# Projecting unnormalised columns that the host laid out, and testing for overfull experts between the last w1 and w3

## The chip, the cores and the metric

The kernel runs on one core of one Trainium2 chip. A core has a matrix engine (PE; its weight loads are listed apart as PEld), a vector engine (DVE), a scalar engine (ACT), a general engine (POOL) and a queue engine (SP) that issues most transfers (DMA). Each engine runs its own list of instructions in order, and semaphores let them wait for each other. The metric is the device time of one execution in microseconds (us); lower is better.

## The reference

One decoder block on 512 tokens of width 1024, in float32, followed by a final norm:

```python
h = rmsnorm(x, attn_norm_w[l])
z = h @ w_in[l]
hq, hf, hi, hg, cq, ckv, kr, gate_a, gate_b = jnp.split(z, split_idx, axis=-1)
...
q = (rmsnorm(c_q, q_norm_w) @ w_uq).reshape(B, S, MLA_HEADS, MLA_QK_DIM)
kv = (rmsnorm(c_kv, kv_norm_w) @ w_ukv).reshape(B, S, MLA_HEADS, MLA_NOPE + MLA_VDIM)
k_pe = apply_rope(k_rope_raw, cos, sin)
...
x = x + y @ w_out[l]
h = rmsnorm(x, ffn_norm_w[l])
x = x + hierarchical_moe(h, ...)
...
y = x * lax.rsqrt(jnp.mean(x * x, axis=-1, keepdims=True) + EPS) * w      # rmsnorm
hid = jax.nn.silu(xb @ w1[e]) * (xb @ w3[e])                              # each expert
return (hid @ w2[e]) * wts[:, None]
```

`cq` has 384 columns and `ckv` with `kr` 320. The mixture of experts has 64 experts of width 512, and each token goes to two. An expert may draw more tokens than one slot list of the kernel holds; it is then called overfull, and a further round has to work off the rest.

## The kernel before

**Order of the work.** The kernel goes through three stages. The *head* (`latent`, L284 to L488) computes the norm, the 384 query columns `cq` and the 320 key and value columns `ckv`/`kr`, and from them the compressed queries (`cqT`), keys (`ckT`) and the values. The *mixers* project and run the latent attention and the recurrent mixer head by head, then the router chooses experts. The *experts* run in 16 blocks of 4 experts each; their weights, 24 MB a block, come through a ring of 22 slots (`RING`) that SP fills as slots come free.

**Products.** A float32 product is made of three reduced-precision ones (`mm3`): each operand is split into a high part (a cast on ACT) and a low part (a subtraction on DVE or POOL), and high by high, high by low and low by high are summed. A tile whose name ends in h or l (`hTh`, `hTl`, `cqwh`, `cqwl`) is such a part.

**The head.** Four tiles of 128 tokens of x are loaded (`xt`). For each one ACT squares it, DVE makes the reciprocal root (`rms_scale`), the tile is scaled, PE transposes it in blocks of 128 (`tr<-dg,xt`, `tr<-cst,xt`), DVE multiplies by the norm's gains (`hf`, L385), ACT casts the high part (`hTh`) and DVE makes the low part (`hTl`, L387). Then PE makes 24 matmuls of 128x384 for this token tile (`c<-cqwh,hTh` and its like: the *query projection*), and after the four tiles 24 of 128x320 a tile (the *key projection*, into `z` and `c`). POOL makes the low parts of the key weights (`ckwl`). The four results are normalised (`xt<-c`), transposed and split into `cqh`/`cql` (`columns`, L429 to L435), and 36 matmuls of 128x512 make the rotary queries (`rotary_queries`, `c<-cqwh,cqh`). After these come the transposes for `ckT`, and then the values (L654, `z<-whi,hTh`).

**The last block of experts.** `block(..., last=True)` makes the 64 matmuls of w1 into `h1`, the 64 of w3 into `h3`, then `spread` (the weights that bring rows back to tokens) and `finish_open`, then the product of both (`t`, DVE L1165), its transposes (`ga<-cst,t`, L1168) and `hid` (ACT L1170). Then `more_rounds` (L1081 to L1085) tests whether an expert is overfull. With these inputs the test is false. On each engine it is a load of the number `ri` into a register (`TENSOR_LOAD`, L1083) and a jump over the body of the overflow rounds (`COMPARE_BRANCH`, L1084), which on PE holds some 230 matmuls:

```python
        nr = nc.values_load(ri[0:1, 0:1], min_val=0, max_val=S // CAP)
        with tc.If(nr > 1):
            self.overflow(Slots(self.pair(len(self.order) + 6)), mps, mp, nr, self.pos, self.e32, self.wts)
```

Then `end` works through w2 in four strips of columns, 512, 256, 128 and 128 wide (`STRIPS`): 16 groups of matmuls into `y`, a copy, four matmuls back to tokens (`cb`, `ga`), additions on DVE, squares on ACT, gains on POOL, and after the last strip the final norm and the stores. SP issues the strips' loads at L887, and passes its own test only after the last of them.

Of the kernel before, what the change touches and what calls it, by code (L numbers as in the profile page):

```python
# [10 lines left out]
F32 = mybir.dt.float32  # L11
# [11 lines left out]
H = 8  # L23
# [53 lines left out]
class Trunk:  # L77
# [48 lines left out]
    def run(self):  # L126
# [3 lines left out]
        nc.scalar.dma_start(out=cst[:, 0:128], in_=a["cf"][:, 0:128])  # L130
# [153 lines left out]
    def latent(self, st, gl, hT, wp):  # L284
# [5 lines left out]
        cqT = [mp.tile([128, 3, S], F32R, name=f"cq{i}") for i in "hl"]  # L290
# [3 lines left out]
        ckT = [mp.tile([128, 2, S], F32R, name=f"ck{i}") for i in "hl"]  # L294
        kpT = [mp.tile([128, S], F32R, name=f"kp{i}") for i in "hl"]
        qpT = mp.tile([128, H, S], F32R, name="qpT")
        scale = float((NOPE + ROPE) ** -0.5)
        with tc.tile_pool(name="c", bufs=1, reuse_waits="tile") as cp, tc.tile_pool(name="cps", bufs=4, space=PSUM, reuse_waits="tile") as cps:
            wk_hl = [cp.tile([128, KT, CW - QR], F32R, name=f"ckw{i}") for i in "hl"]
            gra = cp.tile([8, 128], F32, name="gra")  # L300
            grb = cp.tile([38, 128], F32, name="grb")
            r2 = lambda ap: ap.rearrange("o (k p) -> (o k) p", p=128)
            xt = [cp.tile([128, D], F32, name="xt", bufs=4) for _ in range(T)]

            def load_x(t):
                nc.sync.dma_start(out=xt[t], in_=a["x"][0, t * 128:(t + 1) * 128])

            def weights(c0, w, hl, eng):
                raw = cp.tile([128, KT, w], F32, name="craw")
                hi, lo = hl or [cp.tile([128, KT, w], F32R, name=f"cqw{i}") for i in "hl"]  # L310

                def load(q):
                    nc.sync.dma_start(out=raw[:, 2 * q:2 * q + 2],
                                      in_=w_in[q * 256:(q + 1) * 256, C0 + c0:C0 + c0 + w]
                                      .rearrange("(k p) c -> p k c", p=128))

                def high(kt):
                    nc.scalar.copy(out=hi[:, kt], in_=raw[:, kt])

                def low(kt):  # L320
                    eng.tensor_sub(out=lo[:, kt], in0=raw[:, kt], in1=hi[:, kt])
                return hi, lo, load, high, low

            load_x(0)
            nc.scalar.dma_start(out=gra, in_=r2(a["attn_norm_w"]))
            wq = weights(0, QR, None, nc.vector)
            wq[2](0)
            wq[2](1)
            load_x(1)
            wq[2](2)  # L330
            wq[2](3)
            load_x(2)
            load_x(3)
            wk = weights(QR, CW - QR, wk_hl, nc.gpsimd)
            for q in range(4):
                wk[2](q)
            nc.sync.dma_start(out=self.cst[:, 128:384], in_=a["cf"][:, 128:384])
# [3 lines left out]
            for r0, r1, key in ((0, 16, "hg_lower_bound"), (16, 19, "mla_q_norm_w"), (19, 21, "mla_kv_norm_w"),  # L341
                                (21, 22, "hg_out_norm_w"), (22, 30, "ffn_norm_w")):
                nc.sync.dma_start(out=grb[r0:r1], in_=r2(a[key]))
            nc.sync.dma_start(out=grb[30:38], in_=a["final_norm_w"].rearrange("(k p) -> k p", p=128))
# [4 lines left out]
            ps = cps.tile([128, 8], F32, name="tr", bufs=2)  # L349
            nc.tensor.transpose(ps, gra, ident[0:8, 0:8])  # L350
            nc.vector.tensor_copy(out=gT[:, 0:8], in_=ps)

            def project(ps, w, t):
                ts = slice(t * 128, (t + 1) * 128)
                for kt in range(KT):
                    self.mm3(ps, [hT[0][:, kt, ts], hT[1][:, kt, ts]], [w[0][:, kt], w[1][:, kt]],
                             kt == 0, kt == KT - 1)


            c_sb, cacc = [], []  # L360

            def stats(t):
                return self.rms_scale(sm, xt[t], D, scr)

            def columns_of(t, rs):
                ts = slice(t * 128, (t + 1) * 128)
                if t == 0:
                    dg = cp.tile([128, 128], F32, name="dg")
                    ready = nc.vector.tensor_scalar(out=dg, in0=ident, scalar1=rs, scalar2=None, op0=OP.mult)
                    with tc.issue_after(ready.ins):  # L370
                        for kt in range(4):
                            wq[4](kt)
                else:
                    nc.scalar.activation(xt[t], xt[t], AF.Copy, scale=rs)
                for half in range(2):
                    ps = cps.tile([128, 4, 128], F32, name="tr", bufs=2)
                    for i in range(4):
                        kt = half * 4 + i
                        if t == 0:
                            self.mm(ps[:, i], xt[t][:, kt * 128:(kt + 1) * 128], dg, True, True)  # L380
                        else:
                            nc.tensor.transpose(ps[:, i], xt[t][:, kt * 128:(kt + 1) * 128], ident)
                    ks = slice(half * 4, half * 4 + 4)
# [4 lines left out]
                return cast, low  # L388

            rs = [stats(0)]  # L390
            for kt in range(4):
                wq[3](kt)
            cast, low = columns_of(0, rs[0])
            with tc.issue_after(cast.ins):
                rs.append(stats(1))
                for kt in range(4, KT):
                    wq[3](kt)
            with tc.issue_after(low.ins):
                for kt in range(4, KT):
                    wq[4](kt)  # L400
            for t in range(T):
                if t + 2 < T:
                    rs.append(stats(t + 2))
                if t + 1 < T:
                    cast, low = columns_of(t + 1, rs[t + 1])
                ps = cps.tile([128, QR], F32, name="c")
                project(ps, wq, t)
                cacc.append(ps)
            with tc.issue_after(cast.ins):
                for kt in range(KT):  # L410
                    wk[3](kt)
                    wk[4](kt)
            nc.vector.tensor_copy(out=self.identr, in_=ident)
            for t in range(T):
                rs = self.rms_scale(sm, cacc[t], QR, scr[:, :QR])
                c_sb.append(cp.tile([128, CW - ROPE], F32, name="xt", bufs=4))
                nc.scalar.activation(c_sb[t][:, :QR], cacc[t], AF.Copy, scale=rs)
            kr = cp.tile([128, T, 2, ROPE], F32, name="kr")
            cacc = []
            for t in range(T):  # L420
                ps = zps.tile([128, CW - QR], F32, name="z") if t < 2 else cps.tile([128, CW - QR], F32, name="c")
                project(ps, wk, t)
                cacc.append(ps)
            ps = cps.tile([128, 38], F32, name="tr", bufs=2)
            nc.tensor.transpose(ps, grb, ident[0:38, 0:38])
            nc.vector.tensor_copy(out=gT[:, 8:46], in_=ps)
# [10 lines left out]
            vw = self.value_weights(wp, 0)  # L437
            for r in range(3):
                columns(r, cqT, 0)
            cos, sin = self.angles(cp, pi_)  # L440
            qraw = self.rotary_queries(cp, cps, cqT)
            for t in range(T):
                rs = self.rms_scale(sm, cacc[t][:, :KVR], KVR, scr[:, :KVR])
                nc.scalar.activation(c_sb[t][:, QR:], cacc[t][:, :KVR], AF.Copy, scale=rs)
                nc.scalar.copy(out=kr[:, t, 0], in_=cacc[t][:, KVR:])
# [415 lines left out]
    def prefetch(self, n, eng):  # L861
        goal = min(self.nchunk + n, len(self.order))
        while self.nchunk < goal:
# [12 lines left out]
            elif (i - 16) in self.STRIPS:  # L876
# [3 lines left out]
                n = 512 // w if c0 + w < D else 1  # L880
# [193 lines left out]
    def more_rounds(self, mps):  # L1074
# [9 lines left out]
        with tc.If(nr > 1):  # L1084
            self.overflow(Slots(self.pair(len(self.order) + 6)), mps, mp, nr, self.pos, self.e32, self.wts)  # L1085
# [56 lines left out]
    def block(self, wk, mps, slot, wts, chunk, ready=None, last=False):  # L1142
# [3 lines left out]
        h1 = mps.tile([128, FF], F32, name="h1")  # L1146
        h3 = mps.tile([128, FF], F32, name="h3")
        for i, hp in enumerate((h1, h3)):
            c = chunk(i * 8)
            for kt in range(KT):  # L1150
                for g in range(4):
                    self.mm(hp[32 * g:32 * g + 32], xT[:, kt, 32 * g:32 * g + 32], c(g, kt * 512, 512),
                            kt == 0, kt == KT - 1)
        if ready:
# [161 lines left out]
```

## Time and profile before

| | |
|---|---|
| median of 3 runs | 1607.35 us (1606.48 to 1608.43) |
| the profiled execution | 1605.74 us |
| span of its trace | 1604.0 us (1.74 us lie around it) |
| PE busy, DVE, ACT, POOL | 87%, 37%, 21%, 15% of the span |
| mean transfer rate | 285 GB/s |
| granted PE clock | 0.943 of full speed |

A busy share is a mean over stages with different limits: the head waits for small things, the mixers for PE, most of the expert blocks for transfers. So what an edit is worth is read in its own stage.

### The profile page before, as it was taken

The page shows a single profiled execution, that of the slowest core. Times are in us where ns is not written, and L with a number is a line of the kernel's source. Part 1 is how long each engine was busy: PE and PEld are TensorE (multiplying, and loading weights), DVE is VectorE, ACT ScalarE, POOL GpSimd, SP SyncE. Part 2 cuts the span into 40 slices and gives each one's busy share as a digit, 9 for nine tenths or more (in the row PEclk, how much of TensorE's full clock was granted, in tenths as well). Part 3 has the DMA queues.
Part 4 walks back from the last instruction along what each step waited for, and adds up shares of the span by engine and source line. Part 5 has one row for each costly group of instructions (what it writes and reads, how often), then busy time and mean ns, then how long its engine had stood idle before and what let it go on. Part 6 is the DMA issues. An engine that isn't in the chain of part 4 may idle for free.

```text
span 1604.0 us, 20359 instructions
## 1 busy us (share of the span) xinstructions
PE 1387.9 (87%) x8282; PEld 844.5 (53%) x8282; DVE 592.5 (37%) x1453; ACT 344.6 (21%) x762; POOL 247.8 (15%) x272
## 2 busy tenths in 40 slices
PE   7999999999999999988887788688779779779784
PEld 6878887878788889934243133133223223323322
DVE  7767677686853333621210211111111112012023
ACT  6455523223332223410100000000000000000012
POOL 2021233223000000021111011011012011011012
PEclk9999999999999999998998899898899899889898
DMA  6111222222153338599999999999999999999995
GB/s 219 29 52 51 61 67 66 66 66 66 40 186 104 92 93 328 225 402 430 425 430 429 430 427 428 430 430 427 429 430 429 429 429 429 428 430 428 428 417 175
DMA packets 124766, 456.34 MB, mean 285 GB/s; under 512 B 11854, under 2 KB 93436, under 8 KB 97532
## 3 DMA queue, kind: packets, MB, share of 16 engines
q1 hardware_dynamic: 121852, 454.52, 70.5%
q8 instruction: 67, 1.10, 0.3%
q10 hardware_dynamic: 2816, 0.47, 0.2%
q14 instruction: 31, 0.25, 0.0%
HBM read 452.87 MB, written 2.10 MB: 284 GB/s over the span
## 4 chain that ended last, share of the span: by engine, by line
PE 58%; DMA 26%; DVE 8%; ACT 3%; issue 2%; POOL 1%; SPq 1%; ACTq 0%; POOLq 0%; DVEq 0%
DMA ck<-in_expert_w 24%; PE z L82 13%; PE h L82 10%; PE y L82 10%; PE ga L1111 7%; PE yacc L82 5%; PE wop L82 2%; PE mx L82 2%; PE z L654 1%; PE cb L82 1%; PE sc L82 1%; DVE rs_u L105 1%; PE lv L82 1%; PE o L82 1%; SPq L887 1%
## 5 line engine op out<-in xcount | busy, mean ns | idle before, releaser
L82 PE MATMUL h<-ck,xT 128*32 128x512 f32 x2048 | 311.7, 666 | 123.9 <-DMA ck<-in_expert_w 109.3
L82 PEld LDWEIGHTS h<-ck,xT 128*32 128x32 f32 x2048 | 74.7, 120 | 347.5 <-issue 165.0
L1130 POOL TENSOR_SCALAR t<-cst,slb,wts 128x128 f32<-128x128 f32 x64 | 50.4, 792 | 964.5 <-PE ga L1111 710.0
L1191 DVE TENSOR_TENSOR x<-cb,x 128x512 f32<-128x512 f32 x120 | 83.0, 691 | 290.0 <-PE cb L82 290.0
L82 PE MATMUL y<-ck,hid 128*32 128x512 f32 (+2 forms) x1088 | 171.3, 584 | 16.2 <-ACT hid L1170 9.4
L91 POOL TENSOR_TENSOR wlo<-wraw,whi 128x1024 fp32r<-128x1024 f32 (+3 forms) x52 | 97.6, 1878 | 267.8 <-ACT whi L90 208.2
L82 PE MATMUL z<-hTh,whi 128*128 128x512 f32 x320 | 128.1, 400 | 5.5 <-ACT vh L658 5.4
L1111 PEld LDWEIGHTS ga<-t,wo 128*128 128x128 f32 x1024 | 117.1, 192 | 25.5 <-issue 24.1
L82 PE MATMUL z<-hTh,wlo 128*128 128x512 f32 x320 | 126.9, 397 | 0.0
L82 PE MATMUL z<-hTl,whi 128*128 128x512 f32 x320 | 126.7, 396 | 0.0
L1111 PE MATMUL ga<-t,wo 128*128 128x128 f32 x1024 | 123.2, 278 | 1.2 <-DVE t L1108 1.2
L82 PE MATMUL cb<-xT,owT 128*128 128x512 f32 (+2 forms) x256 | 120.9, 603 | 2.4 <-DVE xT L1207 2.2
L90 ACT CAST whi<-wraw 128x1024 fp32r<-128x1024 f32 (+3 forms) x84 | 77.4, 922 | 173.0 <-PE z L82 93.2
L1165 DVE TENSOR_TENSOR t<-h,t 128x512 f32<-128x512 f32 x16 | 11.1, 692 | 257.9 <-PE h L82 257.9
L82 PEld LDWEIGHTS y<-ck,hid 128*32 128x32 f32 x1088 | 43.7, 111 | 111.2 <-issue 91.6
L82 PEld LDWEIGHTS cb<-xT,owT 128*128 128x128 f32 x256 | 40.3, 188 | 83.5 <-DVE x L1191 46.9
L1187 ACT COPY xT<-y 128x512 f32<-128x512 f32 x30 | 17.6, 585 | 258.5 <-PE y L82 258.5
L1170 ACT COPY hid<-ga 128x512 f32<-128x512 f32 x16 | 9.4, 585 | 293.1 <-PE ga L1168 293.1
L82 PEld LDWEIGHTS z<-hTh,whi 128*128 128x128 f32 x320 | 60.9, 190 | 18.4 <-ACT vh L658 6.0
L1164 DVE TENSOR_TENSOR t<-h,t 128x512 f32<-128x512 f32 x16 | 11.1, 692 | 156.4 <-ACT t L1163 156.4
L82 PEld LDWEIGHTS z<-hTh,wlo 128*128 128x128 f32 x320 | 60.8, 190 | 12.5
L82 PEld LDWEIGHTS z<-hTl,whi 128*128 128x128 f32 x320 | 60.8, 190 | 11.8
(349 smaller groups left out, 2161.2 us busy)
## 6 DMA issues: line engine op xcount, KB each, us to landing
ck<-in_expert_w SPq DMA_DIRECT2D x164, 2048.0 KB, 34.2
ck<-in_expert_w SPq DMA_DIRECT2D x52, 1024.0 KB, 32.4
wraw<-in_w_in SPq DMA_DIRECT2D x48, 512.0 KB, 3.9
wraw<-in_w_branch_mla SPq DMA_DIRECT2D x8, 512.0 KB, 3.7
wraw<-in_w_branch_hgrn SPq DMA_DIRECT2D x8, 512.0 KB, 3.6
wo<-in_w_out SPq DMA_DIRECT2D x8, 512.0 KB, 6.0
xt<-in_x SPq DMA_DIRECT2D x4, 512.0 KB, 6.6
wraw<-in_mla_w_ukv SPq DMA_DIRECT2D x16, 128.0 KB, 2.5
```

Of the source, the lines that this page charges most:

```text
L82: self.nc.tensor.matmul(ps, lhsT=l, rhs=r, start=start, stop=stop)
L90: self.nc.scalar.copy(out=hi, in_=src)
L91: (eng or self.nc.vector).tensor_sub(out=lo, in0=src, in1=hi)
L105: nc.vector.tensor_mul(out=u, in0=u, in1=v)
L654: nc.tensor.matmul(ps[t // 2][:, t % 2], lhsT=L[l], rhs=R[r], start=(kt == 0 and n == 0 and t % 2 == 0), stop=(kt == KT - 1 and n == 2), s ...
L887: eng.dma_start(out=at(ft), in_=w2[ft])
L1111: nc.tensor.matmul(ps[kt // 4][:, kt % 4], lhsT=self.h2[t][:, kt], rhs=oh[:, t], start=(t == 0 and kt % 4 == 0), stop=(t == T - 1), skip_g ...
L1130: nc.gpsimd.tensor_scalar(out=ow[:, t], in0=iota, scalar1=slot(t, 0), scalar2=wts[:, t, 0:1], op0=OP.is_equal, op1=OP.mult)
L1164: nc.vector.tensor_mul(out=sg, in0=rows(h1), in1=sg)
L1165: nc.vector.tensor_mul(out=sg, in0=rows(h3), in1=sg)
L1187: nc.scalar.copy(out=ysb[:, hs], in_=y[half])
L1191: nc.vector.tensor_add(out=self.x2[:, t, hs], in0=ps, in1=self.x2[:, t, hs])
```

## The change

The change has two parts.

**The head.** The host hands in x transposed (`xT`), the two weight slices (`w_cq`, `w_ck`) and all gain vectors (`gains`) in the layout that the chip wants. PE then projects gain times x, without the norm's scale of each token; the scale comes in later, as the scale of the copies that read the results. The loop of the query projection runs over the 8 blocks of 128 features outside and the 4 token tiles inside. x itself is still loaded, for its squares. The normalised `hT`, which the values and later heads need, is made after the key projection from `xT`, gains and the scales spread over all partitions (`rsb`). The low parts of the key weights move from POOL to DVE. The parts of gain times x live in tiles that are free until later (`qpT`, `cqh`, `cql`, `ckh`, and ring slot `ck0` for `xT`).

**The tail.** In the last block `spread`, `finish_open` and `more_rounds` move from behind the matmuls to between those of w1 and those of w3. The overflow body gets other ring slots, since w3 now still stands in the ones that it used, and another PSUM tile for its own `h1`; the last strip packs two pieces into a slot.

```diff
-            def columns_of(t, rs):
...
-                    ps = cps.tile([128, 4, 128], F32, name="tr", bufs=2)
...
-                    hf = cp.tile([128, 4, 128], F32, name="hf", bufs=2)
-                    nc.vector.tensor_mul(out=hf, in0=ps, in1=gT[:, ks, None].to_broadcast([128, 4, 128]))
-                    cast = nc.scalar.copy(out=hT[0][:, ks, ts], in_=hf)
-                    low = nc.vector.tensor_sub(out=hT[1][:, ks, ts], in0=hf, in1=hT[0][:, ks, ts])
...
+            cacc = [cps.tile([128, QR], F32, name="c") for _ in range(T)]
+            for kt in range(KT):
+                g = gT[:, kt:kt + 1]
+                nc.scalar.activation(xgh[:, kt], xT[:, kt], AF.Copy, scale=g)
+                nc.vector.scalar_tensor_tensor(out=low(kt), in0=xT[:, kt], scalar=g, in1=xgh[:, kt],
+                                               op0=OP.mult, op1=OP.subtract)
+                self.split(qraw_[:, kt], wq[0][:, kt], wq[1][:, kt])
+                for t in range(T):
+                    project(cacc[t], wq, t, kt)
...
+            rs = scales([x[:, :] for x in xt], D)
+            for kt in range(KT):
+                self.split(kraw_[:, kt], wk[0][:, kt], wk[1][:, kt])
...
+            sq = scales(cacc, QR, rs)
...
+            for kt in range(KT):
+                hf = cp.tile([128, S], F32, name="hf", bufs=2)
+                nc.vector.scalar_tensor_tensor(out=hf, in0=xT[:, kt], scalar=gT[:, kt:kt + 1], in1=rsb,
+                                               op0=OP.mult, op1=OP.mult)
+                self.split(hf, hT[0][:, kt], hT[1][:, kt])
...
+            sk = scales([c[:, :KVR] for c in cacc], KVR, rs)
...
-                n = 512 // w if c0 + w < D else 1
+                n = 512 // w if c0 + w < D else 2
...
-            self.overflow(Slots(self.pair(len(self.order) + 6)), mps, mp, nr, self.pos, self.e32, self.wts)
+            self.overflow(Slots(self.pair(len(self.order) + 4)), mps, mp, nr, self.pos, self.e32, self.wts)
...
-        for i, hp in enumerate((h1, h3)):
+        hps = []
+        for i in range(2):
+            if i == 1 and last:
+                owT = self.spread(wk, mps, slot, wts)
+                self.finish_open(wk, mps)
+                self.more_rounds(mps)
...
-        owT = self.spread(wk, mps, slot, wts)
-        if last:
-            self.finish_open(wk, mps)
+        if not last:
+            owT = self.spread(wk, mps, slot, wts)
...
-        if last:
-            self.more_rounds(mps)
```

On PE, near the end of the program, the test stood behind the transposes of the product `t`, and the first strip of w2 (`y`) came after the body that it jumps over:

```order
L82 MATMUL h_10108<-ck_9908,xT 32x512 x2
L82 MATMUL h_10108<-ck_9981,xT 32x512 x2
L1168 MATMUL ga<-cst,t_10225 128x128 x4
L1083 TENSOR_LOAD ri
L1084 COMPARE_AND_BRANCH
L1269 COMPARE_AND_BRANCH
```

Now it stands behind the last matmuls of w1 (`h_9998`):

```order
L82 MATMUL h_9998<-ck_9756,xT 32x512
L82 MATMUL h_9998<-ck_9791,xT 32x512
L1041 TENSOR_LOAD ri
L1042 COMPARE_AND_BRANCH
L1232 COMPARE_AND_BRANCH
```

and the rows behind the body begin with those of w3 (`h_10436`), with no jump from there to `y`:

```order
L1042 UNCONDITIONAL_BRANCH
L82 MATMUL h_10436<-ck_9793,xT 32x512 x2
L82 MATMUL h_10436<-ck_9796,xT 32x512 x2
```

So whatever the jump costs PE now lies ahead of w3 and not ahead of w2. On DVE, in the head, the work that makes `hT` stood inside the query projection, tile by tile:

```order
L385 TENSOR_TENSOR hf<-tr,gT 128x512 x2
L102 SCALAR_TENSOR_TENSOR rs_u<-rs_y,rms_v 128x1
L108 TENSOR_SCALAR rs_y<-rms_v 128x1
L387 TENSOR_TENSOR hTl<-hf,hTh 128x4x128
L114 SCALAR_TENSOR_TENSOR rs_y<-rs_u,rs_y 128x1
```

It now stands in one piece between the scales and the splits `cql` that the rotary queries wait for (`ck` is the tile of `xT`):

```order
L91 TENSOR_TENSOR hTl<-hf,hTh 128x512 x2
L377 SCALAR_TENSOR_TENSOR hf<-ck_101,gT,rsb 128x512 x2
L471 TENSOR_SCALAR ang<-ang 128x128
L91 TENSOR_TENSOR cqwl<-craw,cqwh 128x1536
L91 TENSOR_TENSOR hTl<-hf,hTh 128x512 x2
L377 SCALAR_TENSOR_TENSOR hf<-ck_101,gT,rsb 128x512 x2
L388 SCALAR_TENSOR_TENSOR cql<-tr,gT,cqh 128x512
L91 TENSOR_TENSOR hTl<-hf,hTh 128x512 x2
L388 SCALAR_TENSOR_TENSOR cql<-tr,gT,cqh 128x512 x2
```

So the first `cql` is now queued behind six of the eight `hTl` and all eight `hf`.

## Rows read from the trace of the kernel before

**Rows 1.** The page's chain that ended last, by engine and line.

```profile
DMA ck<-in_expert_w 24%; PE z L82 13%; PE h L82 10%; PE y L82 10%; PE ga L1111 7%; PE yacc L82 5%; PE wop L82 2%; PE mx L82 2%; PE z L654 1%; PE cb L82 1%; PE sc L82 1%; DVE rs_u L105 1%; PE lv L82 1%; PE o L82 1%; SPq L887 1%
```

**Rows 2.** Windows: length, busy by engine, then PE clock, transfer share, GB/s.

```profile
400.00:600.00 200.00, 198.42 (x954) 163.15 (x953) 102.94 (x207) 63.98 (x134) 3.56 (x3) 1.00 0.35 103
640.00:660.00 20.00, 19.52 (x167) 19.31 (x166) 9.88 (x49) 8.95 (x18) 0.00 (x0) 1.00 0.50 197
```

**Rows 3.** PE's timeline in the head: start, length, line, operation, idle before.

```profile
5.50 0.24 PE L350 MATMUL tr<-cst,gra 8*128 8x8 f32 x1 [5.50 <-DMA gra<-in_attn_norm_w]
7.98 3.78 PE L82 MATMUL tr<-dg,xt 128*128 128x128 f32 x16 [2.24 <-DVE dg L369]
13.15 0.44 PE L82 MATMUL c<-cqwh,hTl 128*128 128x384 f32 x1 [0.65 <-DVE hTl L387]
...
22.06 0.34 PE L82 MATMUL c<-cqwh,hTh 128*128 128x384 f32 x1
...
25.70 0.34 PE L82 MATMUL c<-cqwh,hTh 128*128 128x384 f32 x1
...
36.21 0.31 PE L82 MATMUL z<-ckwh,hTh 128*128 128x320 f32 x1
...
50.14 0.30 PE L82 MATMUL c<-ckwh,hTl 128*128 128x320 f32 x1
...
54.48 0.79 PE L82 MATMUL c<-cqwh,cqh 128*128 128x512 f32 x1 [0.38 <-ACT cqh L433]
...
64.66 1.03 PE L431 MATMUL tr<-cst,xt 128*128 128x128 f32 x8
65.45 0.36 PE L654 MATMUL z<-whi,hTh 128*128 128x256 f32 x1
```

**Rows 4.** DVE's groups by shape, 0 to 85 us: busy, mean ns, idle before.

```profile
L387 DVE TENSOR_TENSOR hTl<-hf,hTh 128x512 fp32r<-128x512 f32 x8 | 7.2, 906 | 1.5 <-ACT hTh L386 1.4
L385 DVE TENSOR_TENSOR hf<-tr,gT 128x512 f32<-128x512 f32 x8 | 5.3, 684 | 1.2 <-PE tr L82 1.2
```

**Rows 5.** ACT's groups by shape, 0 to 85 us: the load of the exponential's table.

```profile
L483 ACT ACT_TABLE_LOAD x1 | 1.3, 1283 | 0.0
```

**Rows 6.** PE's timeline in the last block.

```profile
1544.29 10.76 PE L82 MATMUL h<-ck,xT 128*32 128x512 f32 x94
...
1559.04 5.32 PE L82 MATMUL h<-ck,xT 128*32 128x512 f32 x26 [1.43 <-DMA ck<-in_expert_w]
1565.23 0.63 PE L1168 MATMUL ga<-cst,t 128*128 128x128 f32 x4 [0.88 <-DVE t L1165]
1572.58 5.39 PE L82 MATMUL y<-ck,hid 128*32 128x512 f32 x32 [6.73 <-DMA ck<-in_expert_w]
```

**Rows 7.** The test's source lines, by engine (q: its sequencer): ns, starts in us.

```profile
L1083 PEldq TENSOR_LOAD <-ri x1: 490/490/490, 1565.2 to 1565.2; - x1
```

```profile
L1084 PEldq COMPARE_BRANCH  x1: 6426/6426/6426, 1565.8 to 1565.8; - x1
...
L1084 ACTq EVENT_SEMAPHORE  x1: 17/17/17, 1570.5 to 1570.5; - x1
```

**Rows 8.** Source line L425 in the head: PE's sequencer and its matmul.

```profile
L425 PEldq EVENT_SEMAPHORE  x2: 51/51/51, 47.7 to 47.8; - x2
...
L425 PE MATMUL tr<-cst,grb x1: 250/250/250, 50.4 to 50.4; 38*128 38x38 f32 x1
```

**Rows 9.** Windows in the last block, columns as in the second group.

```profile
1560.00:1562.00 2.00, 2.00 (x16) 0.50 (x12) 0.00 (x0) 0.00 (x0) 0.00 (x0) 0.50 1.01 387
1568.00:1570.00 2.00, 0.00 (x0) 0.00 (x0) 0.00 (x0) 0.00 (x0) 0.00 (x0) 0.84 1.04 332
...
1581.00:1582.00 1.00, 1.00 (x4) 0.38 (x2) 0.83 (x2) 0.80 (x3) 0.37 (x1) 1.00 0.19 58
```

**Rows 10.** The first strip's last load: its issue (chain), its landing (DMA issues).

```profile
1554.48 2.24 SPq L887
```

```profile
ck<-in_expert_w SPq DMA_DIRECT2D x1, 1024.0 KB, 15.0
```

More of the change, by code (lines that the diff above doesn't have):

```diff
@@ new lines, in latent @@
+            ident, rings = self.ident, self.rings
+            nc.scalar.dma_start(out=gT, in_=a["gains"])
+            nc.scalar.dma_start(out=self.cst, in_=a["cf"][:, 0:384])
+            xT = rings["n"].tile([128, KT, S], F32, name="ck0")
+            xgh = mp.tile([128, H, S], F32R, name="qpT")
+            xgl = [mp.tile([128, n, S], F32R, name=name) for n, name in ((3, "cqh"), (3, "cql"), (2, "ckh"))]
+            low = lambda kt: xgl[kt // 3][:, kt % 3]
+            xt = [cp.tile([128, D], F32, name="xt", bufs=4) for _ in range(T)]
@@ L338, in latent @@
+            wk = [cp.tile([128, KT, CW - QR], F32R, name=f"ckw{i}") for i in "hl"]
+            for k0 in range(0, KT, 4):
+                nc.sync.dma_start(out=kraw_[:, k0:k0 + 4], in_=a["w_ck"][:, k0:k0 + 4])
             nc.sync.dma_start(out=cst2, in_=a["cf"][:, 384:544])
@@ L390, in latent @@
[L390 to L400, printed above, removed]
-            for t in range(T):
[L402 to L413, printed above, removed]
+                self.mm3(ps, [xgh[:, kt, ts], low(kt)[:, ts]], [w[0][:, kt], w[1][:, kt]], kt == 0, kt == KT - 1)
+            cacc = [cps.tile([128, QR], F32, name="c") for _ in range(T)]
[5 more added lines that the diff above has]
+                self.split(qraw_[:, kt], wq[0][:, kt], wq[1][:, kt])
+                for t in range(T):
+                    project(cacc[t], wq, t, kt)
@@ new lines, in scales @@
+            def scales(src, width, rs=None):
+                ss, v = [cp.tile([128, T], F32, name=f"{i}{width}") for i in ("ss", "sv")]
+                for t in range(T):
+                    nc.scalar.activation(scr[:, 0:width], src[t], AF.Square, accum_out=ss[:, t:t + 1])
+                for _ in range(2 if rs is not None else 0):
+                    nc.vector.tensor_mul(out=ss, in0=ss, in1=rs)
+                nc.vector.tensor_scalar(out=v, in0=ss, scalar1=RS / width, scalar2=RS * EPS, op0=OP.mult, op1=OP.add)
+                y = self.rsqrt(sm, v, T)
+                nc.vector.tensor_mul(out=ss, in0=y, in1=rs) if rs is not None else nc.vector.tensor_copy(out=ss, in_=y)
+                return ss
@@ L414, in latent @@
+            rsb = cp.tile([128, S], F32, name="rsb")
+            nc.scalar.copy(out=rsb, in_=ps.rearrange("p t j -> p (t j)"))
+            c_sb = []
+            sq = scales(cacc, QR, rs)
             for t in range(T):
-                rs = self.rms_scale(sm, cacc[t], QR, scr[:, :QR])
                 c_sb.append(cp.tile([128, CW - ROPE], F32, name="xt", bufs=4))
-                nc.scalar.activation(c_sb[t][:, :QR], cacc[t], AF.Copy, scale=rs)
+                nc.scalar.activation(c_sb[t][:, :QR], cacc[t], AF.Copy, scale=sq[:, t:t + 1])
@@ L1140, in spread, with block @@
         return owT
[L1142 removed]
+    def block(self, wk, mps, slot, wts, chunk, ready=None, last=False, other=False):
         nc, ident, iota = self.nc, self.ident, self.iota
         xT = ready or self.gather(wk, mps, slot)
[L1146 to L1148 removed]
+        hps = []
[4 more added lines that the diff above has]
+                self.more_rounds(mps)
+            hp = mps.tile([128, FF], F32, name="cb", bufs=2) if other and i == 0 else \
+                mps.tile([128, FF], F32, name=("h1", "h3")[i])
+            hps.append(hp)
             c = chunk(i * 8)
@@ L1296, with laid_out @@
         "final_norm_w"]
+def laid_out(inputs):
+    rows = lambda m: np.asarray(m).reshape(KT, 128, -1).transpose(1, 0, 2)
+    w = np.asarray(inputs["w_in"])[0]
+    vectors = [np.asarray(inputs[n]).reshape(-1, 128) for n in
+               ("attn_norm_w", "hg_lower_bound", "mla_q_norm_w", "mla_kv_norm_w", "hg_out_norm_w", "ffn_norm_w",
+                "final_norm_w")]
+    return [("xT", rows(np.asarray(inputs["x"])[0].T)), ("w_cq", rows(w[:, C0:C0 + QR])),
+            ("w_ck", rows(w[:, C0 + QR:C0 + CW])), ("gains", np.concatenate(vectors).T)]
 def kernel(**inputs):
```

100 lines of the change are left out of this document (23 added, 77 removed).

## The prediction

> **What bounds the kernel now.** I read the page's chain first. A quarter of the span waits for expert weights, and most of the rest is PE [rows 1]. Then I cut the span into windows. Between 400 and 600 us PE is busy for 198.4 of 200 us, so the mixers run at PE's pace. From 640 to 660 us, in the router, transfers use only half of their time: the ring is full and waits for PE to begin on the experts [rows 2]. So if the head ends earlier, the mixers, the router and the stream of weights all move earlier by the same amount. I read the head from PE's timeline [rows 3] and the costs from the groups of DVE and ACT [rows 4, 5]. I read the tail from PE's timeline in the last block, and from the test's own lines [rows 6, 7].
>
> In the tail the reader should see one thing. The transposes of `t` end at 1565.9, and `hid` follows within 0.6 us, but `y` starts only at 1572.58. The row names a DMA as the releaser. The test's line shows another cause: PE's jump over the overflow body begins at 1565.84 and takes 6.43 us, to 1572.27 [rows 6, 7]. ACT pays too: it is done with `hid` at about 1566.5, and its next instruction, the one behind its jump, is at 1570.5, 4 us later. So the jump stalls its engine.
>
> **The head, step by step.** Before, PE first waits for a small load (5.5 us), then for the norm of the first tile (7.98 to 11.8 are transposes), runs at its full pitch from 13.15 and ends the query projection at 36.2 [rows 3]. The 96 matmuls of 128x384 have a pitch of 0.173 us (21 steps from 22.06 to 25.70), so 16.6 us of that is work; transposes and waits are the rest. The key projection has a pitch of 0.147 (95 steps from 36.21 to 50.14).
>
> After, nothing stands ahead of the first matmul but one block of `xT` and `w_cq`, the gains, and a copy and a cast of 1.1 us on ACT. The gains are a small load like the one that landed at 5.5, so PE starts between 4.5 and 6.6; I take 5.6. Before, 5.2 us went by from PE's first real work to its full pitch. If this holds, PE runs at half rate until 10.8: 15 matmuls of 0.346. The other 81 take 14.0, to 24.8. DVE needs some 1.2 us per block for the two low parts (one 512 wide, at `hf`'s 0.68, and one 384 wide, by its width), less than PE's 2.1, so it is in time. With 0.6 us of friction the query projection ends at 25.4. The key projection takes 14.1, and 0.8 us more because the splits of its weights queue on ACT behind the squares of the results. It ends at 40.3, against 50.3: 10 us earlier.
>
> DVE doesn't keep that. Eight `hf` at 0.68, eight `hTl` at 0.68 to 0.91, one wide split (1.8 by its width), three `cql` (2.2 by the same width and one operand more) and some 25 small operations of 0.2 stand in its list from the scales to the last `cql` [rows 4]: 5.5 + 6.3 + 1.8 + 2.2 + 5 = 20.8 us. They can begin when `rsb` exists, at about 30. So the last `cql` comes at 50.8. The rotary queries (54.48 to 64.66 before [rows 3]) wait for the `cql` one after the other, and PE's clock falls in that wait; they end about 6 us after the last, at 56.8. This is 7.9 us earlier. Then a last chain of twelve small operations and four copies on DVE and ACT stands ahead of the values: about 59.5 against 65.45. I take 5.8 us of gain for the head. Its bounds: 10 if DVE hides everything, 0 if all DVE operations run at the slow end (906/684 = 1.33 times, 6.5 us more).
>
> Two more edits. The load of the exponential's table, 1.28 us [rows 5], stood before the head's chain and now comes at the first softmax, where the mixers wait for ACT at times: I take half, +0.6, bounds 0 and 1.3. The 2 MB of `xT` beside x and the move of `ckwl` to DVE (eight of about 0.5 us) cost nothing of their own: the loads run beside the query projection, and the splits keep ahead of PE's 0.44 us per block and tile but for the friction above.
>
> **The tail, step by step.** The 94 matmuls from 1544.29 start 0.107 us apart (10.76 less some 0.7 for the last one's own length). The first 58 of them are the end of w1, so w1 ends at about 1550.5. PE's sequencer doesn't wait for them. In the head it passed a semaphore at 47.8 whose matmul ran at 50.4, with 17 matmuls of 0.147 in between [rows 8]. At 0.107 per matmul it gets to the test 1.8 us early, at 1548.7. With 0.49 for the load and 6.43 for the jump [rows 7] it is through at 1555.6; `y` began 0.3 us after the jump, so w3 starts at 1555.9. PE has then been idle for 5.5 us. [...] So I let 16 matmuls run at half rate (3.4 us), as in the row from 1559.04, and 48 at 0.107 (5.1): w3 ends at 1564.4. This is where it ends before (1559.04 + 5.32), since before it waits for its own loads; after, these have landed.
>
> From there 2.2 us lead to `y` (the product, transposes, `hid`), at 1566.6, and no jump is left. But the first strip's last load was issued at 1554.48 and landed 15.0 us later, at 1569.5 [rows 10]. SP issues it in the same place as now, so `y` waits for it and ends at about 1570.5, against 1578.0. The strips behind it need their own loads; the transfers end between 1581 and 1582 [rows 9], when the last `y` would start. So the tail brings 7.2 to 7.5 us; I take 7.2. Bounds: with ACT's 4 us in place of 6.43 the same load limits it (7.5). With a jump twice as long w3 ends 6.4 us later, at 1570.8, `y` follows at 1573.0 and takes 3.6 us at the full pitch (32 and one's length): a gain of 1.4. The row is nearest to the new place, so I stay with 6.43.
>
> On the other engines the test stands ahead of work that is needed late: ACT's `silu` of w1 and DVE's products have until 1564. The strip's packing and the overflow's new slots change nothing that runs.
>
> [...]
>
> **The sum.** -5.8 + 0.6 - 7.2 = -12.4. The profiled execution took 1605.74, so 1593.3; the median of the runs is 1.6 above it: **1594.9 us**. The likeliest case's own range is 1592 to 1598.
>
> **Rivals.**
> - *The stall only moves.* w3 ends some 7 us later, because the jump starts only when w1 has ended, lasts longer beside the loads and leaves a cold clock: -5.2 alone, 1602.1. For it speaks that PE stands idle once more ahead of w3; against it, that w3 waits for its loads until 1559.0 anyway.
> - *The head's gain is given back by DVE*, at the slow end above: -6.6 alone, 1600.7. For it speaks the piece of 20.8 us; against it, that the slow `hTl` ran beside POOL's splits, which have become fewer.
> - *PE sets the head after all* (10 us): -16.6, 1590.7.
> [...]
> - *Both gains fail*, and the rest hides the difference: 1607.
>
> **How the numbers follow.** A measurement of this kernel can tell 0.2%, 3.2 us, from no change. Likeliest case 0.55; stall only moves 0.10; DVE gives the head back 0.12; PE sets the head 0.13; both fail 0.05; slower 0.05. The first four are faster: 0.90, same 0.05, slower 0.05. The range takes in the first and the fourth, the third, and the near half of the second: 1590 to 1602.
>
> **What would show it.** Right: query projection done by 26 us, key projection by 41, values from 59 or 60; the jump in front of w3 near 1549 on the old time scale with some 6.4 us, and `y` behind `hid` limited by a load. Wrong: values at 65 with PE idle for DVE; a jump much longer than 8 us; w3 ending after 1567 on that scale; or a mixer stage that doesn't start earlier by what the head saved.

## The result and the profile after

The changed kernel takes 1596.51 us (median of 6 runs, 1594.92 to 1597.65) beside 1607.84 us (6 runs, 1605.35 to 1613.12): a ratio of 0.993, 95% interval 0.9913 to 0.9946. The forecast was 1594.9. The profiled execution took 1594.92 us with a span of 1593.1, 10.8 less than before. The total came out in part by luck: a loss of 3.4 us in the weight stream, which the sum did not have, was made up by 3.4 us more than forecast in the head and the mixers.

**The chain and the windows.** The chain's first part, against [rows 1]:

```profile
DMA ck<-in_expert_w 28%; PE z L82 14%; PE h L82 9%; PE y L82 9%; PE ga L1069 7%; PE yacc L82 5%; PE wop L82 2%; PE c L82 2%; PE mx L82 2%; PE z L612 1%; PE cb L82 1%; PE sc L82 1%; PE o L82 1%; DVE rs_u L105 1%; PE lv L82 1%
```

Waits for weights have grown from 24% to 28%. That is some 60 us, far more than anything that changed, so it shows another path of the chain and not a cost. Windows of the changed kernel (columns as in [rows 2]):

```profile
400.00:600.00 200.00, 198.42 (x943) 163.14 (x942) 96.72 (x186) 61.38 (x121) 3.02 (x2) 1.00 0.38 111
640.00:660.00 20.00, 19.50 (x165) 19.15 (x164) 13.60 (x80) 10.50 (x19) 0.00 (x0) 1.00 0.28 106
```

PE sets the mixers' pace as before, and the ring is still full in the router.

**The head.** PE's timeline of the changed kernel:

```profile
5.55 1.01 PE L82 MATMUL c<-cqwh,qpT 128*128 128x384 f32 x2 [5.55 <-ACT cqwh L90]
...
10.30 0.34 PE L82 MATMUL c<-cqwl,qpT 128*128 128x384 f32 x1
...
24.52 0.34 PE L82 MATMUL c<-cqwh,ckh 128*128 128x384 f32 x1
...
32.91 0.31 PE L82 MATMUL z<-ckwh,ckh 128*128 128x320 f32 x1
37.92 0.64 PE L82 MATMUL c<-ckwh,qpT 128*128 128x320 f32 x1 [4.70 <-ACT xt L366]
...
46.26 0.31 PE L82 MATMUL c<-ckwh,ckh 128*128 128x320 f32 x1
...
57.23 1.16 PE L385 MATMUL tr<-cst,xt 128*128 128x128 f32 x8
...
58.58 0.28 PE L612 MATMUL z<-whi,hTh 128*128 128x256 f32 x1
```

The query projection runs from 5.55 to 24.9 without a gap. The key projection stops for 4.7 us after its second tile: the third needs a PSUM tile `c` that ACT's copies `xt<-c` (L366) free, and they wait for DVE's scales. The row at 58.58 answers to the one at 65.45 in [rows 3]: 6.9 us earlier. (The first three matmuls of the values slip in ahead of it in both traces, at 53.44 before and at 58.14 after, so the mark is the second group.)

**What held DVE.** Its timeline in the changed kernel, then POOL's:

```profile
29.28 0.23 DVE L455 TENSOR_SCALAR ang<-cst,posf 128x32 f32<-128x32 f32 x1
29.42 0.16 DVE L108 TENSOR_SCALAR rs_y<-sv 128x4 int32<-128x4 int32 x1
29.49 2.40 DVE L455 TENSOR_SCALAR ang<-cst,posf 128x32 f32<-128x32 f32 x1
31.81 0.15 DVE L104 TENSOR_TENSOR rs_u<-rs_y 128x4 f32<-128x4 f32 x1
31.89 2.36 DVE L455 TENSOR_SCALAR ang<-cst,posf 128x32 f32<-128x32 f32 x1
```

```profile
29.42 4.79 POOL L91 TENSOR_TENSOR wlo<-wraw,whi 128x1024 fp32r<-128x1024 f32 x2 [29.00 <-ACT whi L90]
```

The same instruction takes 0.23 us, or 2.4. Both long ones start beside a split on POOL and end with it (POOL's pair runs from 29.42 to 34.21, the long rows end at 31.89 and 34.25). The trace of before has the same thing, first on DVE and then on POOL, and the prediction has no term for it:

```profile
39.71 2.37 DVE L102 SCALAR_TENSOR_TENSOR rs_u<-rs_y,rms_v 128x1 f32<-128x1 f32 x1
```

```profile
39.67 2.39 POOL L91 TENSOR_TENSOR wlo<-wraw,whi 128x1024 fp32r<-128x1024 f32 x1 [0.45 <-ACT whi L90]
```

**The tail.** PE's timeline in the last block, then the test's lines:

```profile
1532.90 1.05 PE L82 MATMUL h<-ck,xT 128*32 128x512 f32 x4 [1.04 <-DVE xT L1077]
...
1549.70 4.38 PE L82 MATMUL h<-ck,xT 128*32 128x512 f32 x18 [3.54 <-PEq L1042]
1555.36 5.35 PE L82 MATMUL h<-ck,xT 128*32 128x512 f32 x46 [1.28 <-issue]
1561.60 0.63 PE L1133 MATMUL ga<-cst,t 128*128 128x128 f32 x4 [0.89 <-DVE t L1130]
1562.90 2.78 PE L82 MATMUL y<-ck,hid 128*32 128x512 f32 x24 [0.68 <-ACT hid L1135]
1566.41 1.06 PE L82 MATMUL y<-ck,hid 128*32 128x512 f32 x8 [0.72 <-DMA ck<-in_expert_w]
```

```profile
L1042 PEldq COMPARE_BRANCH  x1: 6192/6192/6192, 1543.2 to 1543.2; - x1
...
L1042 ACTq COMPARE_BRANCH  x1: 54/54/54, 1546.8 to 1546.8; - x1
...
L1042 ACTq EVENT_SEMAPHORE  x1: 17/17/17, 1552.1 to 1552.1; - x1
```

The stall is about as long as in [rows 7] (6.19 us against 6.43). It starts 3.0 us before PE has worked off w1, and leaves PE idle for 3.54 us. ACT's next instruction comes 5.3 us after its own jump, long before ACT is needed for `hid`. The packets of the traces fit a wait for code: one 16 KB packet of the kind "instruction" (queue q8) runs inside the jump, at 1546.89 for 1.10 us here and at 1569.71 for 1.14 us before, and in all thirteen traces with the test the jump ends 1.4 to 1.5 us behind such a packet.

PE stops once more, after 18 matmuls of w3, and the row names no releaser ("issue"). Another such packet ends at 1553.87, and PE goes on 1.5 us later, at 1555.36. All eight traces with the new head and the test in its new place have this stop behind the 18th matmul (0.8 to 2.4 us long), and it ends 1.3 to 1.5 us behind such a packet; e3, without the test, and e1, the same tail in the old program, do not have it. So it looks like a second wait of that kind behind the jump, and not like a wait for weights. No experiment here moves the code alone, so this is read from the times.

`y` follows `hid` by 0.68 us, and its last eight matmuls wait 0.72 us for a load. The granted clock fell to 0.50 of full speed at the start of w3, behind the idle 3.54 us:

```profile
1550.00:1552.00 2.00, 2.00 (x12) 0.45 (x8) 0.00 (x0) 0.00 (x0) 0.00 (x0) 0.50 1.00 391
1552.00:1554.00 2.00, 2.00 (x10) 0.32 (x3) 0.00 (x0) 0.00 (x0) 0.00 (x0) 0.74 1.04 393
```

**The term that was missing.** 700 us of the expert stage in the kernel before, then in the changed one:

```profile
760.00:1460.00 700.00, 567.58 (x3352) 215.98 (x3351) 119.57 (x264) 50.26 (x108) 96.17 (x144) 0.91 1.01 429
```

```profile
760.00:1460.00 700.00, 563.36 (x3330) 214.56 (x3328) 119.50 (x264) 50.35 (x108) 92.59 (x139) 0.91 1.01 427
```

The same transfers, at a transfer share of 1.01, move 427 GB/s in place of 429. The lead over before was 8.6 us at the router's last product and 5.2 at the last block. The change touches no weight load between these points.

### The profile page after: what moved, and what is told of

It is laid out like the page before. It is cut to its first block, busy times and chain, and to the rows that moved or that the text cites. A ratio compares the mean times of both kernels' runs of the same rounds, so it can differ in the third digit from the quotient of the medians.

```text
span 1593.1 us, 20247 instructions
## 1 busy us (share of the span) xinstructions
PE 1377.5 (86%) x8248; PEld 837.8 (53%) x8248; DVE 589.3 (37%) x1420; ACT 347.5 (22%) x768; POOL 240.5 (15%) x264
## 4 chain that ended last, share of the span: by engine, by line
PE 58%; DMA 28%; DVE 8%; ACT 3%; issue 1%; POOL 0%; ACTq 0%; DVEq 0%
DMA ck<-in_expert_w 28%; PE z L82 14%; PE h L82 9%; PE y L82 9%; PE ga L1069 7%; PE yacc L82 5%; PE wop L82 2%; PE c L82 2%; PE mx L82 2%; PE z L612 1%; PE cb L82 1%; PE sc L82 1%; PE o L82 1%; DVE rs_u L105 1%; PE lv L82 1%
## 5 line engine op out<-in xcount | busy, mean ns | idle before, releaser
L82 PE MATMUL y<-ck,hid 128*32 128x512 f32 (+2 forms) x1088 | 168.7, 577 | 10.9 <-ACT hid L1135 10.1
L82 PEld LDWEIGHTS cb<-xT,owT 128*128 128x128 f32 x256 | 40.3, 188 | 83.5 <-DVE x L1154 46.9
L82 PEld LDWEIGHTS z<-hTh,wlo 128*128 128x128 f32 x320 | 60.4, 189 | 12.4
```

The source lines that it names most:

```text
L82: self.nc.tensor.matmul(ps, lhsT=l, rhs=r, start=start, stop=stop)
```

## The experiments

Shifts against the profiled run of the kernel before, in us, from PE's timelines: values (65.45 in [rows 3]), router (the last product of its logits, 674.1 before), last block (first w1, 1538.1 before), end of span. Runs of the kernel before itself spread by some 2 us in these marks.

| | values | router | last block | end | ratio |
|---|---|---|---|---|---|
| changed kernel | -6.9 | -8.6 | -5.2 | -10.8 | 0.993 |
| again (e5) | -5.9 | -7.6 | -4.0 | -9.9 | 0.9945 |
| tail alone (e1) | 0.0 | +0.9 | +0.4 | -4.4 | 0.9954 |
| head alone (e2) | -5.4 | -5.2 | -1.9 | +0.2 | 0.9986 |
| no test (e3) | -5.7 | -5.9 | -0.2 | -7.0 | 0.9944 |
| before, more inputs (e4) | -0.6 | -0.1 | -0.6 | +1.9 | 0.9998 |
| left pad (e6) | -7.0 | -8.5 | -9.1 | -15.8 | 0.9917 |
| angles later (e7) | -1.4 | -3.9 | 0.0 | -6.2 | 0.9967 |
| both of these (e8) | -1.9 | -2.7 | -3.1 | -9.9 | 0.9946 |
| before, shifted (e9) | -1.6 | -1.1 | +2.2 | +4.4 | 1.0039 |
| both pads (e10) | -5.5 | -5.9 | -9.2 | -16.1 | 0.9891 |
| left pad, splits on DVE (e11) | -7.9 | -8.8 | -8.9 | -16.0 | 0.9902 |
| both pads, splits on DVE (e12) | -9.0 | -9.4 | -11.4 | -17.5 | 0.987 |

e1 to e4 ran beside the same runs of the kernel before, and so did e5 to e8 and e9 to e12.

**e1: the tail alone.** The kernel before, with the tail's lines of the diff:

```diff
+            if i == 1 and last:
+                owT = self.spread(wk, mps, slot, wts)
+                self.finish_open(wk, mps)
+                self.more_rounds(mps)
```

> The kernel before with the tail's part of the change alone. My steps: the jump starts before w1 has ended, w3 ends where it ended before, the first strip's last load limits y, so 7.2 us less than before (1600 to 1601). Rival from the trace of the changed kernel: there the loads of w3 and of the first strip came about 2 us later against PE than before, and y ended only 5.4 us earlier on the old scale. If that lateness belongs to the tail's edit itself, this kernel gains 5.4 (1602); if it comes from the weight stream after a faster head, it gains 7 or more here and its stream keeps 429 GB/s.

Ratio 0.9954, interval 0.9937 to 0.9971: 4.7 to 10.1 us. At the old rate of the stream `y` starts at 1566.10, where the prediction had put it (1566.6):

```profile
1555.13 8.77 PE L82 MATMUL h<-ck,xT 128*32 128x512 f32 x64 [3.42 <-DMA ck<-in_expert_w]
1566.10 3.05 PE L82 MATMUL y<-ck,hid 128*32 128x512 f32 x24 [0.68 <-ACT hid L1177]
1570.78 1.06 PE L82 MATMUL y<-ck,hid 128*32 128x512 f32 x8 [1.63 <-DMA ck<-in_expert_w]
```

**e2: the head alone.** The changed kernel, with the tail as before:

```diff
-            if i == 1 and last:
-                owT = self.spread(wk, mps, slot, wts)
-                self.finish_open(wk, mps)
-                self.more_rounds(mps)
...
+        if last:
+            self.more_rounds(mps)
```

> The kernel before with the head's part alone; the test stands in its old place. My forecast for the head was 5.2 us less (1602). The trace of the changed kernel shows the router 8.6 us earlier but the last block only 5.2 earlier. If a slower weight stream (427 in place of 429 GB/s) belongs to the head's part, this kernel shows 427 too and gains about 5 us; if it was chance in that run, it shows 429 and gains 8 to 9 (1599).

Ratio 0.9986, interval 0.9976 to 0.9995, at most 3.9 us where about 5 were expected. Of the head's 5.4 us 5.2 arrive at the router and 1.9 at the last block, close to the 2.2 us by the medians; the stream runs at 427 GB/s. So the head's edits bring the slower stream. The two parts alone sum to 0.994, as the whole.

**e3: no test.** The changed kernel without `more_rounds` (the test and the overflow rounds are left out):

```diff
-                self.more_rounds(mps)
```

> The changed kernel without the test for overfull experts (it leaves out the rounds that would work them off; with these inputs there are none). If the jump is hidden, as I forecast, because w3 and y then wait for loads, this gains at most 1.5 us on the changed kernel. If the 6.2 us of the jump still stand on PE's path, it gains 4 to 6.

Ratio 0.9944, interval 0.9928 to 0.9961; the changed kernel has 0.9945 in e5. From the last block's start to `y` go 29.0 us, against 30.0 in the changed kernel and 29.7 in e5. So the jump in its new place, with the stop behind it, costs 0.7 to 1 us on this way. The rest is hidden: 3.0 us lie under w1's last matmuls, and w3 would have to wait for its loads, as it does in e3 once the jump is gone:

```profile
1557.06 1.04 PE L82 MATMUL h<-ck,xT 128*32 128x512 f32 x2 [1.45 <-DMA ck<-in_expert_w]
1559.61 5.11 PE L82 MATMUL h<-ck,xT 128*32 128x512 f32 x26 [1.51 <-DMA ck<-in_expert_w]
```

This run says less than it should, as its code also moved the ring's slots (below).

**e4: four more inputs.** The kernel before also declares the host's four arrays, unused:

```diff
-    for name, arr in [(n, inputs[n]) for n in _INS] + [("cf", cf), ("cm", cm)]:
+    for name, arr in [(n, inputs[n]) for n in _INS] + [("cf", cf), ("cm", cm)] + laid_out(inputs):
```

> The kernel before with the four extra host arrays declared as inputs but never loaded. Nothing on any engine changes, so it should take the time of before. If the stream's rate hangs on where the arrays lie in memory, this kernel shows 427 GB/s in the expert blocks and takes 3 to 4 us more; if not, 429 and the same time.

Ratio 0.9998, 429 GB/s: where the inputs lie in memory is not the cause.

**What was left for the stream.** The records of single packets between 800 and 1400 us, with the address in a partition at which the compiled programs place the ring's slots:

```
                     16 KB packets: mean ns, share up to 612, 613-618, from 619   8 KB: mean   left slots from   right slots from
before               613.9          70%   21%    8%                               310.0        4352 (0 mod 256)   111584 (224 mod 256)
changed              616.6          25%   51%   24%                               314.2        4224 (128)         111584
no test (e3)         617.3           6%   65%   28%                               314.6        4064 (224)         111584
left pad (e6)        614.1          70%   22%    8%                               309.0        4352 (0)           111584
before, shifted (e9) 616.5          25%   51%   24%                               314.6        4480 (128)         111584
both pads (e10)      612.5         100%    0%    0%                               309.0        4352 (0)           111360 (0)
```

The new head no longer needs `rms_scale`'s small tiles for these steps. Their pool shrinks from 616 to 488 bytes per partition, and every tile behind it on the left side, half of the ring among them, moves down by 128 bytes. An estimate: 16 KB packets that take 0.44% longer cost 3.8 us over the 870 us of the stream.

**e5 and e6: the changed kernel again, and with the left slots moved back.** e6 pads a constant tile by 128 bytes, of which nothing is used:

```diff
-        cst = const.tile([128, 384], F32, name="cst")
+        cst = const.tile([128, 416], F32, name="cst")
```

> The changed kernel once more, as the measure for the three kernels beside it on the same chip: about 0.993 of before, 427 GB/s in the expert blocks.

> The changed kernel with the first constant tile 128 bytes longer, which moves every weight slot on the left side of the memory back to the address that it had before. In the kernels with the old head a 16 KB packet of weights mostly took 611 ns, in those with the new head 614 to 621. Theory: the head's smaller scale tiles moved the slots by 128 bytes, and the packets' time hangs on the address they are written to. Then this shows 429 GB/s, packets of 611 ns, and takes 3 to 4 us less than the changed kernel. Rival: the rate hangs on something else of the new head (order of lanes, an extra 2 MB load); then 427 and no difference.

0.9945 (0.9932 to 0.9959) and 0.9917 (0.9903 to 0.9931): 4.6 us by the medians, and 429 GB/s. The lead of 8.5 us at the router is 9.1 at the last block. The packets take their old times again (table above). So the address of the slots is the cause of the slower stream.

**e7 and e8: DVE's angles behind the query scales**, without and with the left pad, so that the long instructions of the head's timeline would no longer stand between the scales:

```diff
-            cos, sin = self.angles(cp, pi_)
+            with self.tc.issue_after(scaled.ins):
+                cos, sin = self.angles(cp, pi_)
```

> The changed kernel with the angle operations of DVE issued after the scales of the query results. In the changed kernel two of them took 2.4 us each while POOL worked on a split, ahead of the chain that the third key tile waits for (PE idle for 4.7 us). Theory: the wait goes, the key projection ends some 4 us earlier and the values start 2 to 4 us earlier; of that 1 to 3 us reach the end. Rival: DVE's whole piece of work, not this chain, sets the rotary queries; then PE waits as long a little later and nothing is gained.

> Both edits together: the slots at their old addresses and the angles later. If both theories hold, 5 to 7 us less than the changed kernel, about 0.989 of before.

Worse: 0.9967 (0.9955 to 0.998) and 0.9946 (0.9932 to 0.9959) against 0.9945 and 0.9917. The theory that the angles hold up the scales fell. DVE's timeline of e7, then its POOL's, then PE's list of waits (total, times, longest):

```profile
30.80 2.26 DVE L104 TENSOR_TENSOR rs_u<-rs_y 128x4 f32<-128x4 f32 x1
33.10 2.31 DVE L105 TENSOR_TENSOR rs_u<-rs_u,sv 128x4 f32<-128x4 f32 x1
```

```profile
30.64 4.74 POOL L91 TENSOR_TENSOR wlo<-wraw,whi 128x1024 fp32r<-128x1024 f32 x2 [30.22 <-ACT whi L90]
```

```profile
PE c L82 <- ACT xt L367: 3.9, 1, 3.9
PE c L82 <- DVE cqwl L91: 3.7, 1, 3.7
```

What DVE runs beside these two splits is held again, now the scales themselves. And the split `cqwl` has moved behind the `cql`, a new wait of 3.7 us.

**e9: the kernel before with the same pad**, which there moves the left slots off the multiple of 256:

```diff
-        cst = const.tile([128, 384], F32, name="cst")
+        cst = const.tile([128, 416], F32, name="cst")
```

> The kernel before with one constant tile lengthened by 128 bytes in each partition; nothing else is changed. Every tile allocated behind it on the left side of SBUF moves by 128 bytes, the left-hand slots of the weight ring among them (from 4,352, a multiple of 256, to 4,480, which is none). Theory (the slots' address sets the rate of the weight stream): the stream falls from 429 to 427 GB/s, the 16 KB packets go from 611 ns to 614 and 621 ns, and the time rises by 3 to 5 us, ratio 1.002 to 1.003. Rival (the address is only a companion of the padded kernel's gain, which came from something else in the changed kernel): 429 GB/s and a ratio of 1.000.

Slower, 1.0039 (1.0026 to 1.0053), at 427 GB/s and with the changed kernel's packet times: 128 unused bytes cost the kernel before 4.2 to 8.5 us, where 3 to 5 were expected.

**e10: both pads.** A pad of 224 bytes on the right side as well:

```diff
+        self.wk.tile([128, 56], F32, name="pad")
```

> The changed kernel with the 128-byte pad on the left and a pad on the right, so that all four slots of the weight ring begin at multiples of 256. Theory (only addresses that are multiples of 256 take 611 ns a packet): the 614 and 621 ns packets that are left with the left pad alone (a quarter of them) go, the stream reaches 429 to 431 GB/s and the time lies 0 to 4 us below that of the left pad alone, ratio 0.989 to 0.992. Rival (the slots on the right never cost anything): the ratio of the left pad alone, 0.992, and the same packets.

0.9891 (0.9876 to 0.9906), against 0.9917 (0.9903 to 0.9931) with the left pad alone: the intervals just touch. All packets take the short time, and the stream moves 430 GB/s:

```profile
760.00:1460.00 700.00, 568.81 (x3392) 218.54 (x3385) 119.49 (x264) 50.94 (x109) 99.01 (x150) 0.91 1.01 430
```

**e11 and e12: the first head's splits on DVE**, with the left pad and with both:

```diff
-                           self.nc.gpsimd) for kp in range(KT // 4)]
+                           self.nc.vector if h == 0 else self.nc.gpsimd) for kp in range(KT // 4)]
```

> The changed kernel with the left pad, and with the splits of the first head's value weights on DVE in place of POOL. Theory (POOL's 4.8 us split holds up whatever DVE instruction runs beside it, so that the chain of the query scales and PE's third key tile come late): no DVE instruction of the head takes 2.3 us any more, PE's wait of 4.7 us at the key projection falls to 1 to 2 us, the values start 2 to 3 us earlier, ratio 0.990 to 0.9915 against 0.992 for the pad alone. Rival (two splits of 1024 elements on DVE take as long from its piece as POOL took): values not earlier, ratio 0.992 or above.

> Both pads, and the first head's splits on DVE. If both theories hold, the gains add: 1 to 3 us below the two pads alone, ratio 0.987 to 0.991. If the splits on DVE give nothing, the ratio of the two pads; if the right-hand slots cost nothing, the ratio of the left pad with the splits on DVE.

DVE's groups in e11, 0 to 85 us, show no held instruction (the four `ang` had a mean of 1309 ns in the changed kernel), and PE's wait shrinks:

```profile
L91 DVE TENSOR_TENSOR wlo<-wraw,whi 128x1024 fp32r<-128x1024 f32 x2 | 2.4, 1216 | 0.0
...
L455 DVE TENSOR_SCALAR ang<-cst,posf 128x32 f32<-128x32 f32 x4 | 0.9, 236 | 0.0
```

```profile
PE c L82 <- ACT xt L366: 2.7, 1, 2.7
PE c L82 <- ACT cqh L387: 1.4, 1, 1.4
```

The hold is shown. Its price is smaller than expected (a wait of 1 to 2 us and values 2 to 3 us earlier): the wait falls from 4.7 to 2.7 us, and the values start 0.9 us earlier in e11 than in e6. In e12 they start 3.5 us earlier than in e10, but most of that is the clock. Windows of the key projection in e10, then in e12:

```profile
38.00:41.00 3.00, 3.00 (x11) 3.00 (x12) 2.93 (x7) 3.00 (x6) 0.00 (x0) 0.50 0.00 0
41.00:44.00 3.00, 3.00 (x13) 3.00 (x13) 3.00 (x5) 1.59 (x4) 0.00 (x0) 0.51 0.00 0
```

```profile
38.00:41.00 3.00, 3.00 (x23) 3.00 (x22) 3.00 (x8) 3.00 (x6) 0.00 (x0) 1.00 0.22 66
41.00:44.00 3.00, 3.00 (x23) 2.99 (x22) 3.00 (x5) 0.40 (x3) 0.00 (x0) 1.00 0.00 0
```

In e10 22 matmuls ran at half rate, 0.12 us longer each, 2.6 us together; an estimate of the splits' own worth is then about 1 us in both pairs. They take 2.4 us of DVE in return. Ratios 0.9902 (0.9887 to 0.9917) and 0.987 (0.9855 to 0.9885). e12 against e11 gives the right-hand slots, 0.3%; e12 against e10 and e11 against e6, the splits, have overlapping intervals. e12, at 1586.05 us, is the fastest kernel here, by the medians some 0.6% below the changed one.

## Why the prediction was right, and where it was not

**The query projection was right.** PE starts at 5.55 (predicted 5.6), reaches full pitch at 10.3 (10.8) and is done at 24.9 (25.4).

**"It ends at 40.3" failed.** The key projection ends at 46.4. The step took ACT's splits as the only friction. It did not ask when the PSUM tiles of the query projection come free: there are four `c`, the third key tile needs one, and it waits for the query scales, for 4.7 us. POOL's hold on DVE makes these scales late: without it (e11, e12) the wait is 2.7 us. The granted clock then fell (0.51 from 38 to 41 us), and the next 11 matmuls had a pitch of 0.267 in place of 0.147, another 1.3 us.

**"The head, 5.8 us" held, but not by the stated mechanism.** The times came out: the last `cql` is done at 51.5 (predicted 50.8), the rotary queries at 57.2 (56.8), and the values start 5.4 to 7.0 us earlier in the six runs with this head, unaltered besides pads (5.8 taken). The step that failed is "20.8 us" of DVE from 30 on. From the end of the hold, at 34.2, to the last `cql` DVE works for only some 16 us: the eight `hTl` take 684 ns each, and the small operations in this stretch some 2 us in place of 5. POOL's hold of some 4.3 us, which was not in the sum, put the loss back. And DVE was not alone the bound: the first `cql` needs transposes that stand behind the key projection in PE's list. In all six runs the last `cql` is done 5.1 us after the key projection (46.4 and 51.5 here, 47.9 and 53.0 in e2), and DVE stands idle for 1.2 to 2.6 us in between and just before. So the two errors, a piece too long and a key projection too early, offset each other. That is luck.

DVE's rows in the changed kernel, and its group of `hTl` (0 to 85 us):

```profile
47.77 0.75 DVE L388 SCALAR_TENSOR_TENSOR cql<-tr,gT,cqh 128x512 fp32r<-128x512 f32 x1 [0.87 <-ACT cqh L387]
48.85 1.29 DVE L91 TENSOR_TENSOR hTl<-hf,hTh 128x512 fp32r<-128x512 f32 x2 [0.34 <-ACT hTh L90]
50.06 1.40 DVE L388 SCALAR_TENSOR_TENSOR cql<-tr,gT,cqh 128x512 fp32r<-128x512 f32 x2
```

```profile
L91 DVE TENSOR_TENSOR hTl<-hf,hTh 128x512 fp32r<-128x512 f32 x8 | 5.2, 684 | 0.3 <-ACT hTh L90 0.3
```

The table load (+0.6) shows no cost: between values and router these kernels gain between -0.2 and 1.7 us more, while e1, e4 and e9, with the old head, lose 0.5 to 0.9. Where the gain comes from stays open.

**"The mixers, the router and the stream of weights all move earlier by the same amount" failed in its last part.** Mixers and router did. The stream gave back 3.4 us (8.6 to 5.2; 3.6 in e5, 3.3 in e2), because the change moved the ring's left slots by 128 bytes. No step looked at the layout of SBUF, and no rival was about it. e6 and e9 show it from both sides. With the old addresses (e6) the same change ends near 1591, at 0.9917.

**The tail was right in mechanism**, against the rival that the stall only moves. On the old scale (5.2 us of lead at the last block) the jump begins at 1548.4, predicted 1549.2 (1548.7 and the load of 0.49), and w3 starts at 1554.9 (1555.9). That 16 matmuls run at half rate behind an idle 5.5 us is shown by no run, as none is idle that long ahead of w3; after the changed kernel's 3.54 us the clock stood at 0.50 from 1550 to 1552 on its own scale and w3's first 18 matmuls took 4.38 us, and after the 3.33 us of e12 they took 2.73. The stop of 1.3 us behind its 18th matmul was not in the sum, and w3 ends at 1565.9 (1564.4). `y` follows `hid`, and the first strip's last load ends it, as forecast, at 1572.7 (1570.5). From the last block's start to the end of the span go 65.9 us before, 60.2 after: 5.7 where 7.2 was forecast. In e6, at the old addresses, it is 59.2, a gain of 6.7, so about 1 us of the miss goes with the later loads. The rest is within the spread of runs: with the test in its old place e2, e4 and e9 take 67.9, 68.4 and 68.1, so the trace of before is a short one; with the test in its new place the seven runs e5 to e8 and e10 to e12 take 58.8 to 59.9.

By the profiled executions the terms are: values -6.9 (-5.8 forecast), mixers -1.7 (+0.6), stream +3.4 (none), tail -5.7 (-7.2), together -10.9 where -12.4 was forecast.

## What to carry to other kernels

When a change adds or drops tiles, compare the addresses of the tiles that a bandwidth-bound stream writes; here a pad that puts the left ones back at multiples of 256 was worth 4.6 us, nearly as much as the head (5.4 to 7.0 at the values). Before you price an engine's piece of work, look at how long one and the same instruction takes at different times: a row of ten times the usual length (2.40 us in place of 0.23 here) that ends with a row of another engine points to what holds it. For each group of matmuls that is moved forward, ask who frees its PSUM tile. And where a jump moves, look for a second stop in the code behind it.

## What the runs showed of the hardware

- The time of a DMA packet went with the address in SBUF that it wrote. With all slots of the ring at multiples of 256 bytes (e10) the share of 16 KB packets up to 612 ns rounds to 100%; with none there (changed kernel, e9) 25% took that, 51% 613 to 618 and 24% 619 or more. The means are 612.5 (e10), 616.6 with slots at 128 and 224 mod 256 (changed kernel), 0.7% more, and 617.3 with all at 224 (e3), 0.8% more; for 8 KB packets they are 309.0, 314.2 and 314.6. Of the weight loads the pads move only the side that is written, and no run here measures transfers that read at such addresses in SBUF.
- Beside a split of 128x1024 on POOL, 2.4 us, one DVE instruction took until the split's end: `ang`, else 0.23 us, took 2.40 and 2.36 (changed kernel), and `rs_u`, else 0.16, took 2.26 and 2.31 (e7).
- The jump over a body of some 230 matmuls took PE's sequencer 6.43 us before and 6.19 in the changed kernel, and 6.0 to 6.5 in the thirteen traces that have it, in either place. ACT's next instruction came 4 us after its own jump before and 5.3 us after it in the changed kernel, though the branch itself took 54 ns in both.
- After an idle stretch of 4.7 us PE's granted clock fell to 0.5, in the changed kernel and e6 until about 41 us, in e2 and e10 until about 44; after one of 2.7 us it fell in e11 (0.50 from 38 to 41 us) and not in e12 (1.00). The values start 1.5 us later in e10 than in e6, whose heads have the same instructions; an estimate: 11 more matmuls at half rate, 0.12 us longer each, are 1.3 us of that.
